# Encoder layer: where TensorE's idle warming products stand

## The chip, the cores and the metric

The kernel runs on one core of a Trainium2 chip. The metric is device time in microseconds: from one launch to its end, median over runs. One core has five engines that run their own instruction streams and wait for each other through semaphores: TensorE (PE; its weight loads are listed as PEld), VectorE (DVE), ScalarE (ACT), GpSimd (POOL) and SyncE (SP), the last of which here only issues DMAs.

## The reference

One encoder layer over a sequence of 4096 tokens of width 1024, all in float32:

```python
h = rmsnorm(x, pre_norm_g)
q, k, v, g_a, u_p, g_p = split(h @ w_in)          # 1024 -> 2304 columns
a = banded_attention(q, k, v, rel_bias, sink) * silu(g_a)   # |i-j| <= 128, 8 heads, 2 kv heads
p = multiscale_pool(u_p, pool_w, pool_scale) * silu(g_p)    # windows 2, 4, 8, 16
x = x + rmsnorm(concat(a, p) @ w_out, post_norm_g)
```

The products carry float32 as pairs of float16 (a high and a low part), three products for one: high by high, low by high, high by low.

## The kernel before, in words

The layer is worked off in two stages. The first makes the projections for the gates and the pooling channels (the columns g_p, g_a and u_p) for eight token tiles of 512 tokens and writes their results to scratch memory; it also scales and splits all weights. The second makes q, k and v, the attention and the output product. Only the very start of the first stage is touched by the change.

Every piece of work is a small function that is entered into a plan with a due time, `due(t, function, ...)`. At the end of the stage the plan is sorted by these times and each function issues its instructions in that order, so the due times alone set the order of the instructions within each engine's stream. They are not times at which anything runs: an instruction runs when it is at the head of its engine's stream and what it waits for is done.

The start, in the order of its data:

- SP loads the gain `g_pre`, four blocks of 128 tokens of x, and the weight tiles 0 and 2 (`x_load` L191, `w_load` L353).
- `gain_square` (L366) makes `gg`, the squared gain, on VectorE. `w_square_raw` (L406) squares a raw weight tile on ScalarE, and `w_norm_raw` (L415) lets TensorE sum these squares with `gg` as the stationary operand: 8 products of 128 x 128 for each of the two weight tiles. From their maximum `pair_scale` (L132 to L148) makes the power of two by which the weights are scaled.
- `row_prod` (L615) is one float32 product on TensorE for the attention's relative bias; `row_keep` (L619) copies it out of its PSUM buffer.
- `w_high` (L482, ScalarE) and `w_low` (L485, VectorE) write the two float16 parts of a scaled weight tile into `wa`.
- `x_high` (L224, ScalarE) and `x_low` (L231, VectorE) write the two parts of a normalised token block, and `x_turn` (L238) has SP issue the DMA that transposes it into `xt`.
- `mm_block(si, i)` (L926) makes the product of weight tile `si` with token block `i`: 24 products of 128 x 128 with 128 moving columns. The order is (0, 0), (0, 1), (2, 0), (2, 1), then, once token block 2 has been turned, (0, 2), (2, 2), (0, 3), and a last (2, 3). These eight blocks are the first products of the layer proper.

`warm_up` (L908) is neither input nor output of any of this. It multiplies constant ones with a part of `gg` and leaves the result in a PSUM buffer that nobody reads. It shares three PSUM buffers (the tag "wup") with the bias product and with the products of `u_prod` (L387), which come later. Its stationary operand `ones16` is set by VectorE with the kernel's first instructions (L161).

In the plan, `w_norm_raw` is due at 10.4 and 11.5, `row_prod` at 11.7, `warm_up` at 11.8 and the first `mm_block` at 16.3.

## Time and profile before

| | |
|---|---|
| median of three runs | 1167.52 us (1167.19 to 1174.55) |
| the profiled execution's own time | 1169.97 us |
| its span, first to last instruction | 1168.2 us |
| mean granted TensorE clock | 0.998 |
| busy: TensorE, VectorE, ScalarE, GpSimd | 97%, 79%, 65%, 25% |

All views below are of that one profiled execution. Times in them are microseconds from the span's start; an engine's busy time is a share of the span. A timeline row gives the start, the duration, the engine, the line of the kernel, the operation with the tile it writes and the tiles it reads, their shapes, how many instructions were merged, and in brackets the idle time ahead of it and what ended it. In a row of stretches the number behind x counts the instructions that ran in the stretch, also those cut by its edges.

### The profile page before, as it was taken

The page shows a single profiled execution, that of the slowest core. Times are in us where ns is not written, and L with a number is a line of the kernel's source. Part 1 is how long each engine was busy: PE and PEld are TensorE (multiplying, and loading weights), DVE is VectorE, ACT ScalarE, POOL GpSimd, SP SyncE. Part 2 cuts the span into 40 slices and gives each one's busy share as a digit, 9 for nine tenths or more (in the row PEclk, how much of TensorE's full clock was granted, in tenths as well). Part 3 has the DMA queues.
Part 4 walks back from the last instruction along what each step waited for, and adds up shares of the span by engine and source line. Part 5 has one row for each costly group of instructions (what it writes and reads, how often), then busy time and mean ns, then how long its engine had stood idle before and what let it go on. Part 6 is the DMA issues. An engine that isn't in the chain of part 4 may idle for free.

```text
span 1168.2 us, 30455 instructions
## 1 busy us (share of the span) xinstructions
PE 1132.3 (97%) x12528; PEld 839.2 (72%) x12528; DVE 920.6 (79%) x1890; ACT 757.4 (65%) x1696; POOL 286.5 (25%) x270
## 2 busy tenths in 40 slices
PE   6999999999999999999999999999999999999997
PEld 4548888888888888887576676667666666766643
DVE  5788787778878986957887778778778778777896
ACT  5756666666565535166687767777677777777773
POOL 1000000000000000001454444454444444544322
PEclk9999999999999999999999999999999999999999
DMA  9577898786988956999899999899789889898877
GB/s 262 151 238 271 202 262 286 270 301 214 316 248 264 251 203 174 342 285 251 204 188 203 219 221 203 181 235 209 158 224 217 183 220 210 206 210 213 176 186 217
DMA packets 312635, 265.00 MB, mean 227 GB/s; under 512 B 214528, under 2 KB 275584, under 8 KB 303792
## 3 DMA queue, kind: packets, MB, share of 16 engines
q1 hardware_dynamic: 308464, 248.38, 78.2%
q0 software_dynamic: 4032, 14.68, 7.2%
q8 instruction: 98, 1.61, 0.6%
q14 instruction: 41, 0.34, 0.1%
HBM read 132.97 MB, written 79.21 MB: 182 GB/s over the span
## 4 chain that ended last, share of the span: by engine, by line
PE 43%; DMA 4%; DVE 3%; ACT 1%; issue 1%; SPq 0%; DVEq 0%; POOLq 0%; ACTq 0%
PE ms L1963 11%; PE aq_p L1750 9%; PE m L1963 8%; PE o L1831 4%; PE s L1531 4%; PE kv L1492 3%; PE kv L1712 3%; DMA xt<-x_scr 2%; DMA pt<-pn 2%; PE z L1935 1%; DVE pn L1604 1%; DVE p_all L1549 1%; PE s L1935 0%; DVE mo L2005 0%; SPq L1613 0%
## 5 line engine op out<-in xcount | busy, mean ns | idle before, releaser
L989 PEld LDWEIGHTS <-wa 128*128 128x128 f16 x3360 | 329.5, 98 | 45.9 <-issue 7.3
L989 PE MATMUL ch<-xt,wa 128*128 128x256 f16 x1920 | 214.2, 274 | 3.7 <-ACT cbig L1001 3.7
L1560 ACT ACTIVATE p_all<-p_all,nm 128x384 f32<-128x384 f32 (+1 forms) x256 | 152.4, 596 | 41.1 <-DVE nm L1549 41.1
L1604 DVE SCALAR_TENSOR_TENSOR pn<-p_all,rd,pn 128x384 f16<-128x384 f32 (+1 forms) x256 | 144.5, 624 | 37.0 <-ACT pn L1596 36.2
L1963 PE MATMUL ms<-wo,ys 128*128 128x512 f16 x720 | 165.4, 379 | 3.0 <-DVE ys L1869 0.8
L1596 ACT ACTIVATE pn<-p_all,rd 128x384 f16<-128x384 f32 (+1 forms) x256 | 134.6, 596 | 35.7 <-DVE rd L1582 16.3
L1549 DVE CUSTOM_DVE_ANT_0 p_all<-s,ybig,nsink 128x384 f32<-128x384 f32 (+1 forms) x256 | 155.7, 664 | 1.7 <-PE s L1531 1.7
L1963 PEld LDWEIGHTS <-ys 128*128 128x128 f16 x720 | 68.8, 98 | 84.0 <-issue 2.4
L1963 PE MATMUL m<-wo,y 128*128 128x512 f16 x540 | 124.0, 379 | 0.3 <-DVE mo L2005 0.2
L989 PE MATMUL cl<-xt,wa 128*128 128x256 f16 x960 | 106.9, 273 | 2.2 <-DVE cbig L1014 1.7
L1869 POOL TENSOR_TENSOR y<-yf,y 128x512 f16<-128x512 f32 x29 | 33.6, 1159 | 272.4 <-ACT y L1865 272.4
L1750 PEld LDWEIGHTS <-raw 128*128 128x128 f16 x864 | 83.3, 98 | 17.4 <-issue 4.8
L1963 PEld LDWEIGHTS <-y 128*128 128x128 f16 x540 | 51.6, 98 | 61.4 <-issue 1.5
L210 POOL TENSOR_SCALAR ssq<-ssq 128x4 f32<-128x4 f32 (+1 forms) x11 | 5.5, 500 | 349.5 <-ACT jk L201 343.6
L302 DVE TENSOR_TENSOR xt<-ybig,xt 128x1024 f16<-128x1024 f32 x56 | 67.2, 1218 | 15.3 <-ACT xt L297 15.3
L1750 PE MATMUL aq_p<-xt,raw 128*128 128x256 f16 x672 | 78.1, 273 | 0.4 <-issue 0.4
L1831 PE MATMUL o<-pt,vv 128*64 128x256 f16 x1128 | 68.4, 274 | 1.8 <-DMA pt<-pn 1.7
L1869 POOL TENSOR_TENSOR ys<-at,ys 128x512 f16<-128x512 f32 x28 | 33.8, 1208 | 147.9 <-ACT ys L1865 124.3
L1831 PEld LDWEIGHTS <-vv 128*64 128x64 f16 x1128 | 59.2, 110 | 14.3 <-issue 14.3
L1531 PE MATMUL s<-k_all,q 64*32 64x288 f16 (+7 forms) x3432 | 63.1, 265 | 1.5 <-ACT k_all L1480 1.0
L1023 ACT ACTIVATE gp<-cbig,cg 128x256 f32<-128x256 f32 x42 | 19.0, 499 | 68.7 <-DVE cbig L1014 68.7
L2000 POOL TENSOR_TENSOR mo<-mo,ybig 128x512 f32<-128x512 f32 x39 | 51.3, 1316 | 44.4 <-ACT jkb L1989 44.2
(207 smaller groups left out, 1934.1 us busy)
## 6 DMA issues: line engine op xcount, KB each, us to landing
x_scr<-xt SPq DMA_DIRECT2D x16, 1024.0 KB, 7.5
xt<-x_scr SPq DMA_DIRECT2D x16, 1024.0 KB, 9.3
xn<-in_x SPq DMA_DIRECT2D x28, 512.0 KB, 8.0
ybig<-in_xT SPq DMA_DIRECT2D x28, 512.0 KB, 6.9
y_scr<-xt SPq DMA_DIRECT2D x14, 1024.0 KB, 7.0
xt<-y_scr SPq DMA_DIRECT2D x14, 1024.0 KB
mo<-in_x POOLq DMA_DIRECT2D x28, 512.0 KB, 7.4
out<-mo SPq DMA_DIRECT2D x28, 512.0 KB
```

Of the source, the lines that this page charges most:

```text
L302: eng.tensor_tensor(out=o[:, w, 1], in0=y_view(i), in1=o[:, w, 0], op=ALU.subtract)
L989: nc.tensor.matmul(acc[:, c], wa[:, q, wi, slot * HK + k, c * P : (c + 1) * P], x[:, xi, k, :], start=(fresh and n == 0), stop=(n > 3 * 2 ...
L1531: nc.tensor.matmul(s_bank[jj][r0 : r0 + nr, gg, c0:c1], q_t[u, half][a, qi, jj, tl + r0 : tl + r0 + nr], k_all[a, ki, kc : kc + c1 - c0], ...
L1549: nc.vector.tensor_tensor_reduce(out=p_t[b, half][:, hh, :nk], in0=s_t[b, half][jj][:, gg, :nk], in1=bias[:, h, lo : lo + nk], scale=negc[ ...
L1560: nc.scalar.activation(p[:, hh, :nk], p[:, hh, :nk], AF.Exp, bias=nm_t[b, half][:, hh : hh + 1], scale=-1.0, accum_out=den_t[b, half][:, h ...
L1596: nc.scalar.activation(prob_view(b, half)[:, 0, i], p_t[b, half][:, i, :nk], AF.Copy, scale=rd_t[b, half][:, 0, i : i + 1],)
L1604: nc.vector.scalar_tensor_tensor(out=pn4[:, 1, i], in0=p_t[b, half][:, i, :nk], scalar=rd_t[b, half][:, 0, i : i + 1], in1=pn4[:, 0, i], o ...
L1750: nc.tensor.matmul(acc[:, jj], w[:, wi, jj, k, :], x[:, xi, k, :], start=(first and n == 0), stop=(last and n > 3 * 2 * HK - 3), skip_grou ...
L1831: nc.tensor.matmul(o_ps[a, 2 * half : 2 * half + 2], v[:, vi, kt, a], pt[b, half][:, pi, g, :, i, :], start=(n == 0), stop=(n == last),)
L1869: eng.tensor_tensor(out=y[:, :, 1], in0=f(u), in1=y[:, :, 0], op=ALU.subtract)
L1963: nc.tensor.matmul(z_t[u, tag], y[:, k, yi, :], wo[o][:, wi, k, :], start=(n == 0 and acc is None), stop=(n == 3 * HK - 1), skip_group_che ...
L2000: eng.tensor_tensor(out=mo, in0=mo, in1=gpost[:, cs], op=ALU.mult)
```

## The change

Two things change in `warm_up` and its place. It had been six products that stream 512 columns of `gg`; it becomes forty products that stream the 128 columns of the ones themselves, into a buffer of 128 columns. Its due time goes from 11.8 to 0.6, which puts it at the head of TensorE's stream, ahead of the norm products and of the bias product. It no longer reads `gg`.

```diff
         def warm_up():
 
-            junk = psa.tile([P, 512], F32, name="warm", tag="wup", bufs=3)
-            for n in range(6):
-                nc.tensor.matmul(junk, ones16, gg[:, :4], start=(n == 0), stop=(n == 5))
+            junk = psa.tile([P, P], F32, name="warm", tag="wup", bufs=3)
+            for n in range(40):
+                nc.tensor.matmul(junk, ones16, ones16, start=(n == 0), stop=(n == 39))
...
         due(11.7, row_prod)
-        due(11.8, warm_up)
+        due(0.6, warm_up)
         due(21.0, row_keep)
```

## The prediction

> **What bounds the kernel now.** I read the page first: busy shares, slices, chain that ended last.

> ```profile
> PE 1132.3 (97%) x12528; PEld 839.2 (72%) x12528; DVE 920.6 (79%) x1890; ACT 757.4 (65%) x1696; POOL 286.5 (25%) x270
> ...
> PE   6999999999999999999999999999999999999997
> ...
> PE 43%; DMA 4%; DVE 3%; ACT 1%; issue 1%; SPq 0%; DVEq 0%; POOLq 0%; ACTq 0%
> ```

> TensorE is busy for 97% of the span, and the chain is mostly its matmuls. Only the first slice (29.2 us) falls to 6 tenths, and the change lies wholly in it. So the question is whether a shift there is handed on to the rest. Next I read the timeline of TensorE over the start (start, duration, engine, line, operation, idle time before it and its releaser).

> ```profile
> 10.56 1.96 PE L415 MATMUL n<-sq,gg 128*128 128x128 bf16 x16 [10.56 <-ACT sq L406]
> 12.45 1.87 PE L615 MATMUL fp<-onehot,rbias 32*8 32x512 f32 x2
> 14.25 2.74 PE L908 MATMUL warm<-gg,ones 128*128 128x512 bf16 x6
> 16.79 6.93 PE L926 MATMUL gp<-xt,wa 128*128 128x128 f16 x96
> 24.27 4.18 PE L926 MATMUL gp<-xt,wa 128*128 128x128 f16 x72 [0.55 <-DMA xt<-cbig]
> ```

> The six warming products stand directly ahead of the first 96 products, which are four blocks of 24: channel tiles 0 and 2 with the token blocks 0 and 1. Then TensorE is out of work for 0.55 us until token block 2 has been transposed. That wait at 24.27 is the **gate of the start**: whatever is gained ahead of it must be gained against a DMA that does not depend on the warming.

> The speed of TensorE has to be read from how many products begin in a stretch, because the column of the granted clock reads 1.00 from the first microsecond on, also where the spacing is double (columns: stretch, its length, busy time and matmuls of TensorE, granted clock, DMA share, GB/s).

> ```profile
> 16.79:19.73 2.94, 2.94 (x29) 1.00 1.12 249
> 19.73:23.55 3.82, 3.82 (x71) 1.00 1.28 210
> ...
> 12.90:16.31 3.41, 3.41 (x7) 1.00 1.07 228
> ...
> 231.35:234.77 3.42, 1.35 (x13) 1.00 0.92 355
> 234.77:238.18 3.41, 3.13 (x15) 0.50 1.01 284
> 238.18:241.59 3.41, 3.41 (x34) 1.00 1.07 367
> ```

> Two or three products at the left edge of a stretch began before it. So about 27.5 began in 2.94 us, 0.107 us each, and about 68.5 in 3.82 us, 0.056 us each: the rate doubles at 19.73, in the middle of the 96. The same halving is written in the clock column later: after a stretch in which TensorE was busy for 1.35 of 3.42 us the clock is 0.50 for exactly one stretch of 3.41 us, then 1.00 again. 19.73 + 63 x 3.4133 = 234.77, so both changes lie on one grid of 3.41 us; I take it that the clock is decided once per grid stretch from how busy that stretch was. It opened after 3.13 busy of 3.41 (92%). It did not open at 16.31, although TensorE counts as busy throughout 12.90 to 16.31: that stretch held two products with 32 active rows and 8 columns, and only 2.06 us (60%) of full warming products, from 14.25.

> **The change part by part.**

> *Removed: six 512-wide products ahead of the first product.* They hold TensorE from 14.25 to 16.79, 2.54 us. What is late next? The first product needs its weight and the transpose of token block 0.

> ```profile
> 13.79 1.15 ACT L482 ACTIVATE wa<-raw,sc 128x1024 f16<-128x1024 f32 x1 [0.25 <-DVE sc L148]
> ...
> 15.01 1.28 DVE L485 SCALAR_TENSOR_TENSOR wa<-raw,sc,wa 128x1024 f16<-128x1024 f32 x1
> ...
> 9.80 1.89 SPq L238 DMA_TRANSPOSE xt<-cbig  x1
> ...
> 12.96 3.59 SPq L238 DMA_TRANSPOSE xt<-cbig  x1
> ...
> 17.51 6.26 SPq L238 DMA_TRANSPOSE xt<-cbig  x2
> ```

> The high half of the weight is written at 13.79 + 1.15 = 14.94; the low half (15.01 + 1.28 = 16.29) is wanted only after 16 products. So block 0 starts at about 15.05 instead of 16.79, if its transpose has landed. And the blocks behind it? These are the transpose's issue-to-landing time (one transpose, token block 2, has it) and the DMA packets in five short stretches; a transpose moves packets under 512 bytes, the loads larger ones.

> ```profile
> DMA to landing us min/median/max: 6.7/6.7/6.7
> ...
> DMA packets 313, 0.08 MB, mean 200 GB/s; under 512 B 313, under 2 KB 313, under 8 KB 313
> ...
> DMA packets 6, 0.02 MB, mean 61 GB/s; under 512 B 0, under 2 KB 0, under 8 KB 6
> ...
> DMA packets 449, 0.11 MB, mean 287 GB/s; under 512 B 449, under 2 KB 449, under 8 KB 449
> ...
> DMA packets 14, 0.06 MB, mean 115 GB/s; under 512 B 0, under 2 KB 0, under 8 KB 14
> ...
> DMA packets 20, 0.08 MB, mean 137 GB/s; under 512 B 0, under 2 KB 0, under 8 KB 20
> ```

> In order: 13.0 to 13.4 (block 0 moving), 14.0 to 14.4 (done), 17.0 to 17.4 (block 1 moving), 18.2 to 18.7 and 18.7 to 19.3 (done). Token block 2 landed at 17.51 + 6.7 = 24.2, which is the wait seen at 24.27. Block 0 landed between 13.4 and 16.79, where its products began; by its packets at about 14.2. Block 1 landed between 17.4 and the beginning of its products: 24 x 0.107 after 16.79, 19.35. I take **18.8**, behind the end of its packets.

> So after the change block 0 runs 15.05 to 17.62 (or from 16.5, if a transpose always took 6.7 us; nothing below changes), TensorE waits about 1.2 us for block 1, and the other 72 products run from 18.8 on. That is half a microsecond earlier than in the profile (19.35), not 1.74. At full speed they would take 72 x 0.056 = 4.0 us and end at 22.8, with 1.4 us to spare before 24.27. At half speed throughout they would end at 18.8 + 72 x 0.107 = 26.5. What counts is when the clock opens.

> *Added: forty 128-wide products in the first microseconds.* Their operand is ready when DVE has set the ones.

> ```profile
> 0.86 0.17 DVE L161 MEMSET ones<- 128x128 bf16 x1
> ...
> L908 PEld LDWEIGHTS <-ones 128*128 128x128 bf16 x6 | 0.7, 136 | 2.8 <-issue 2.8
> ...
> L415 PE MATMUL n<-sq,gg 128*128 128x128 bf16 x16 | 2.0, 307 | 10.6 <-ACT sq L406 10.6
> ```

> So they begin near 1.1; at 0.107 us each they take 4.3 us and end near 5.4, at full rate sooner. TensorE has nothing else until 10.56, so they cost nothing. The ends for the unseen length: 40 x 0.056 = 2.2 us, and, were they not overlapped at all, 40 x 0.307 = 12.3 us, ending at 13.4 and holding back the norm products queued behind them (10.56) by 2.8 us; that begins to cost from 0.237 us each. The norm products, 16 of the same shape in 1.96 us with a wait inside, say 0.12 or less, so I take 0.107. No DMA and no instruction of another engine is moved; in TensorE's own order the burst passes 16 norm products and the bias product. PSUM buffers: warming and bias product swap two of three buffers; the next taker of each comes after 29 us, long after both are read. Nothing there.

> *What the burst leaves behind.* From 5.4 to 10.56 TensorE idles for 5.2 us. In the row 231.35:234.77 an idle 2.07 us inside one grid stretch closed the clock; 5.2 us put at least 2.6 idle into one stretch, so a clock opened by the burst is closed again by about 10 us wherever the grid lies.

> [...]

> *The sum.* The clock is closed when the products begin. In this profile's grid the stretches end at 19.73 and 23.14. Between 16.31 and 19.73 TensorE would work 1.31 + 0.93 = 2.24 us (66%), close to the 60% that did not open; so it opens at 23.14. By then (23.14 - 18.8)/0.107 = 40.6 of the 72 are done; 31.4 x 0.056 = 1.76 more give 24.90, against 24.27: **+0.63 us**. The grid's place at the start is free. If a stretch must be 92% busy, the opening falls between 21.9 and 25.3, and the same sum gives +0.06 to +1.7; with a full stretch up to 25.6, +1.8. The middle is about **+0.9**.

> Is it handed on? The next waits of TensorE that another engine ends last are these.

> ```profile
> 49.77 5.14 PE L939 MATMUL a<-xt,wa 128*128 128x512 f16 x23 [0.93 <-DVE wa L485]
> ...
> 55.85 0.38 PE L426 MATMUL n<-wsq,ones 128*128 128x2 f32 x2 [0.94 <-ACT wj L422]
> ```

> The first hangs on weights scaled by a norm that TensorE made at 44.08, so the delay arrives there as well; between zero and all of it passes, and I take all.

> So the profiled execution, 1169.97 us for a span of 1168.2, becomes 1170.9. It lies 2.45 above the median of the three runs, 1167.52 (1167.19 to 1174.55). On the median: **1168.4 us**, +0.08%. A measurement of this kernel can tell about 1%, 11.7 us, from no change; this is far inside.

> **The rivals.**

> *The clock opens in time: 1167.5.* If 66% of a stretch is enough, it opens at 19.73 here, and by 21.9 in any grid, the 72 products end before 24.27, and the DMA gate gives the same time as before. For: no row lies between 60% and 92%. Against: 66% is nearer to the stretch that failed. Chance 0.29.

> *The open clock outlives the gap: 1167.3.* The norm products run at 0.056, their end comes at most 0.4 us earlier, of which ACT's wait of 0.25 before 13.79 is all that the weight and the later transposes can use: -0.25. Chance 0.03.

> *The start is TensorE-bound: 1165.8.* If the wait at 24.27 came from work that follows TensorE, all 16.79 - 15.05 = 1.74 us would be won. Against: the row names the transpose, and the 6.7 us explain it. Chance 0.05.

> ```profile
> 53.86:57.28 3.42, 2.48 (x13) 1.00 1.24 19
> 57.28:60.69 3.41, 3.41 (x18) 1.00 0.37 22
> ```

> *Slower, the clock closes in the new wait: 1169.2.* If it is open by 18.8, the 72 products end at 22.8 and TensorE idles 1.4 us, 42% of a stretch. A stretch with 61% idle closed it; the stretch 53.86 to 57.28 above, with 0.94 of 3.42 us idle (27%), was followed by one at 1.00. Then the products from 24.27 run at half rate for up to 3.41 us, a loss of 1.7. It decides from an idle share of some 45%, and needs the grid to lie so. Chance 0.08.

> **How the numbers follow.** The forecast (0.0 to +1.8) has 0.50, the rivals 0.29, 0.03, 0.05 and 0.08, and 0.05 is left for what I do not see. None of the cases reaches 1%, so nearly all falls within it: 0.02 faster, 0.95 within, 0.03 slower. The range: below, the TensorE-bound start, 1165.8; above, the same cases on an execution like the profiled one, 1169.97 + 1.8 = 1171.8, and with the closing clock 1169.97 + 1.7 + 1.8 = 1173.5. Two of the four times of before (1169.97, 1174.55) lie well over the median, so I go to 1173.0.

> **What would show it.** Right: forty short products from about 1.1, ended by 5.5; a first block from about 15.05; a wait for the transpose of block 1 until 18.8; some 30 to 60 more products at 0.107 spacing, so that the 72 end later than 24.27; the wait at 24.27 gone or the block after it late by under 2 us; everything from 60 us on shifted by one constant. Wrong: a later start of the norm products than 10.56 (burst too long), a spacing of 0.056 already at 15 us (the clock stayed open), or a change that grows along the span.

## The result

| | before | changed |
|---|---|---|
| median | 1168.26 us (1166.43 to 1174.55, 14 runs) | 1171.11 us (1168.55 to 1173.94, 14 runs) |
| ratio to before | | 1.0024 (95% interval 1.0015 to 1.0033) |
| the profiled execution: time, span | 1169.97, 1168.2 us | 1170.10, 1168.3 us |

The change makes the kernel 2.8 us slower (1.75 to 3.9), a quarter of one per cent. The two profiled executions differ by 0.13 us only: that of before lies 1.7 above its median, that of the changed kernel 1.0 below. So the pair of profiles can show what happens at the start, but not the whole difference.

This is TensorE's timeline over the start of the changed kernel.

```profile
1.09 3.73 PE L908 MATMUL warm<-ones 128*128 128x128 bf16 x40 [1.09 <-DVE ones L161]
10.61 1.96 PE L415 MATMUL n<-sq,gg 128*128 128x128 bf16 x16 [5.79 <-ACT sq L406]
12.50 1.87 PE L615 MATMUL fp<-onehot,rbias 32*8 32x512 f32 x2
15.03 2.74 PE L926 MATMUL gp<-xt,wa 128*128 128x128 f16 x24 [0.67 <-ACT wa L482]
18.86 10.82 PE L926 MATMUL gp<-xt,wa 128*128 128x128 f16 x144 [1.09 <-DMA xt<-cbig]
...
57.08 0.38 PE L426 MATMUL n<-wsq,ones 128*128 128x2 f32 x2 [0.94 <-ACT wj L422]
```

The forty products run from 1.09 to 4.82, then TensorE idles for 5.79 us. Block 0 starts at 15.03 instead of 16.79, but TensorE then waits 1.09 us for the transpose of block 1. The wait for the transpose of block 2 (0.55 before) is gone: TensorE arrives there late. The norm product (L426) which had begun at 55.85 begins at 57.08, **1.23 us late**; "late" is meant here and below against the one profiled execution of before. TensorE's speed explains it (columns: stretch, length, busy time and matmuls of TensorE, granted clock, DMA share, GB/s).

```profile
0.50:3.91 3.41, 2.82 (x27) 1.00 0.51 121
3.91:7.32 3.41, 0.91 (x16) 1.00 1.01 405
...
14.15:17.56 3.41, 2.74 (x25) 0.50 0.98 259
17.56:20.98 3.42, 2.33 (x23) 0.50 1.11 259
20.98:24.39 3.41, 3.41 (x35) 0.50 1.32 171
24.39:27.80 3.41, 3.41 (x64) 1.00 1.09 294
```

Here the burst opened the clock at 3.91: ahead of it a product takes about 0.104 us (27 in 2.82 us), behind it 0.057 (16 in 0.91 us). From there on the column goes with the spacing: 0.50 where 35 products are counted in 3.41 us, 1.00 where 64 are. The stretch from 3.91 to 7.32 holds 0.91 us of work, and the clock closes at its end, more than 3 us before the norm products. It stays closed for five stretches, 7.32 to 24.39; the column reads 0.50 in all five. Without the two or three at the left edge that began before, the products take about 0.107 us each in 20.98 to 24.39 and about 0.056 in the next stretch.

The stretch from 14.15 to 17.56 is busy for 2.74 us (80%), and the clock does not open at its end. The first 0.22 us of that are the end of the bias product; this is the same stretch for the products of `mm_block` (L926) alone:

```profile
14.15:17.56 3.41, 2.53 (x24) 0.50 0.98 259
```

What becomes of the 1.23 us? First the same view for the rest of the span, before and changed:

```profile
57.28:1160.00 1102.72, 1086.30 (x12158) 1.00 0.87 227
```

```profile
57.28:1160.00 1102.72, 1086.79 (x12164) 1.00 0.86 228
```

TensorE is busy for 0.49 us more behind the start, which is little. Next, TensorE's timeline near 149 us, before and changed:

```profile
149.17 2.78 PE L989 MATMUL cl<-xt,wa 128*128 128x256 f16 x24 [1.22 <-DVE cbig L1014]
152.03 8.02 PE L989 MATMUL ch<-xt,wa 128*128 128x256 f16 x72
```

```profile
144.76 7.16 PE L989 MATMUL cl<-xt,wa 128*128 128x256 f16 x63
152.00 8.02 PE L989 MATMUL ch<-xt,wa 128*128 128x256 f16 x72
```

Up to here the changed kernel is late by the same amount: a cast of ScalarE that waits for TensorE (L297) begins at 145.15 before and at 146.38 changed. In the kernel before, TensorE then waits 1.22 us for VectorE (L1014, which runs from 148.43 there and from 148.40 in the changed kernel). The changed kernel has no wait there, and at 152 the two are level: in this pair the whole 1.23 us are taken up. Later waits move the two against each other again: at 177.53 the kernel before waits 1.03 us for ScalarE, and the changed kernel, which does not, has begun these products at 175.90, now 1.6 us early. Near 235 both wait for ScalarE and go on 0.24 us apart, before and changed:

```profile
235.05 1.22 PE L989 MATMUL ch<-xt,wa 128*128 128x256 f16 x5 [2.35 <-ACT cbig L1001]
```

```profile
234.81 1.39 PE L989 MATMUL ch<-xt,wa 128*128 128x256 f16 x11 [3.74 <-ACT cbig L1001]
```

### The profile page after: what moved, and what is told of

Read it like the earlier page. It is cut to its first block, busy times and chain, and to the rows that moved or that the text cites. A ratio compares the mean times of both kernels' runs of the same rounds, so it can differ in the third digit from the quotient of the medians.

```text
span 1168.3 us, 30522 instructions
## 1 busy us (share of the span) xinstructions
PE 1135.4 (97%) x12562; PEld 844.1 (72%) x12562; DVE 922.0 (79%) x1890; ACT 757.7 (65%) x1696; POOL 284.9 (24%) x270
## 4 chain that ended last, share of the span: by engine, by line
PE 42%; DMA 5%; DVE 3%; ACT 1%; issue 1%; SPq 1%; DVEq 0%; POOLq 0%; ACTq 0%
PE ms L1963 11%; PE aq_p L1750 8%; PE m L1963 8%; DMA xt<-x_scr 4%; PE o L1831 4%; PE s L1531 4%; PE kv L1492 3%; PE kv L1712 3%; PE z L1935 1%; DMA pt<-pn 1%; DVE pn L1604 1%; DVE p_all L1549 1%; PE s L1935 0%; SPq L1613 0%; DVE mo L2005 0%
```

## The experiments

**Theory A**: the loss is the clock that is closed when block 1 begins; the early burst has no part in it, since it is forgotten by 10 us. **Rivals**: the burst itself costs (B); the form costs, forty short instead of six wide (E); a delay at the start grows on the way (C) or is taken up (D); block 0's early start costs (F). All ratios are to runs of the kernel before that belong to the same comparison.

| run | what is different | ratio (95%) | the norm product of 55.85 begins at |
|---|---|---|---|
| changed kernel | | 1.0024 (1.0015 to 1.0033) | 57.08 |
| e1_none | no warming at all | 1.0026 (1.0013 to 1.0038) | 56.95 |
| e2_both | early burst and the six wide ones | 0.9999 (0.9989 to 1.0009) | 56.39 |
| e3_short_old | forty short ones, old place | 1.0003 (0.9990 to 1.0016) | 56.87 |
| e5_late32 | before, 32 more behind the fourth block | 1.0014 (1.0004 to 1.0025) | 56.47 |
| e5_late64 | the same, 64 | 1.0020 (1.0010 to 1.0030) | 57.64 |
| e8_late180 | the same, 180 | 1.0053 (1.0034 to 1.0072) | 64.67 |
| e6_fill_wait | changed, 12 full products in the wait for block 1 | 0.9990 (0.9975 to 1.0005) | 56.11 |
| e10_thin | changed, 12 thin products there | 1.0015 (1.0001 to 1.0030) | 58.84 |
| e7_open | TensorE filled from 1.1 us on | 1.0004 (0.9989 to 1.0019) | 58.75 |
| e9_again | changed kernel again | 1.0020 (1.0009 to 1.0031) | 56.52 |
| e9_look2, e9_look3 | changed kernel, one execution each | 1171.26, 1173.12 us | 55.90, 56.21 |

### No warming, and both

```diff
-        due(11.8, warm_up)
```

> The warming products are taken out altogether. Theory A (the clock is closed when the products begin, and the early burst has no part in it): TensorE behaves as in the changed kernel, block 0 from 15.0, a wait for block 1 until 18.9, the clock opens between 21.9 and 25.6, the second norm product after the start (57.08 in the changed kernel, 55.85 before) between 55.9 and 57.7; time as the changed kernel, about 1171, ratio to before 1.0015 to 1.0033. Rival B (the forty products, their place or their instructions cost something themselves): the time falls back to that of before, 1168.3, ratio 0.999 to 1.001.

Without any warming the ratio is that of the changed kernel, 1.0026. The medians say less: 1171.37 us of 12 runs against 1170.56 us of 35, only 0.8 us apart; the means are 2.5 us apart, since four of the 12 runs lie between 1174 and 1177. TensorE's stretches in the profile:

```profile
17.11:20.53 3.42, 2.30 (x23) 1.00 1.14 271
20.53:23.94 3.41, 3.41 (x35) 1.00 1.16 228
23.94:27.36 3.42, 3.42 (x64) 1.00 1.21 171
```

The clock opens at 23.94, as late as in the changed kernel (the column reads 1.00 ahead of it too, so the opening is read from the counts, 35 products and then 64). So the early burst is worth nothing here: without it the clock opens no later, at 23.94 against 24.39.

```diff
+        due(0.6, warm_early)      # the forty products
         due(11.8, warm_up)        # the six wide ones
```

> The forty early products are added and the six wide ones stay where they were. Theory A: as before, the first product at 16.8, the clock open between 17.7 and 21.1, the wait for the transpose at 24.27 still there, ratio 0.999 to 1.001. Rival B (the early burst itself costs): as the changed kernel, ratio 1.0015 to 1.0033.

0.9999: the burst costs nothing either, B falls. So what the changed kernel lacks is the six wide products just ahead of block 0. In this execution the transpose of block 2 came late, as its timeline shows:

```profile
24.78 4.18 PE L932 MATMUL gp<-xt,wa 128*128 128x128 f16 x72 [1.59 <-DMA xt<-cbig]
```

And the three stretches around that wait:

```profile
18.63:22.05 3.42, 3.42 (x64) 1.00 1.31 163
22.05:25.46 3.41, 1.81 (x34) 1.00 0.98 207
25.46:28.87 3.41, 3.41 (x64) 1.00 0.98 249
```

The clock opened at 18.63 and stayed open although TensorE was busy for only 1.81 of 3.41 us (53%).

### The form alone

```diff
-            for n in range(6):
-                nc.tensor.matmul(junk, ones16, gg[:, :4], ...)
+            for n in range(40):
+                nc.tensor.matmul(junk, ones16, ones16, ...)
```

> Only the form changes: the forty 128-wide products stand at the old place, behind the bias product. Theory A (what counts is whether TensorE is dense in the microseconds before the 72 products of blocks 1 and on): dense from 14.3, the burst ends between 17.9 and 18.6, the clock opens between 17.1 and 20.9, the 72 products end between 23.5 and 25.0, so 0 to +0.8 us, ratio 0.9995 to 1.001. Rival E (the form is what costs, 40 short instead of 6 wide): as the changed kernel, ratio 1.0015 to 1.0033.

1.0003: the place costs, not the form, though the interval (to 1.0016) just touches what E expects. The norm product is 1.02 us late in this profile, more than the 0 to 0.8 us that I expected.

### A delay of known size

```diff
         due(11.8, warm_up)
+        due(21.0, fill, 32)       # 64, 180: idle products behind the fourth block
```

> The kernel before with 32 idle products of 128 columns between the fourth and the fifth block: 32 x 0.056 = 1.8 us of work at 23.5, of which 0.55 to 0.7 fill the wait for the transpose; the rest, 1.1 to 1.2 us, is a delay of known size at 24.27 with the clock open. Handed on whole: ratio 1.0010, 1169.4. Rival C (a delay at the start grows on the way, since the changed kernel is 2.8 slower by the median with 1.2 in the one profile): 1170.5 or more, ratio 1.002 or more. Rival D (later waits take it up): under 0.5 us, ratio below 1.0005.

> The same with 64 idle products: 64 x 0.056 = 3.6 us, a delay of 2.9 to 3.0 us at 24.27. Handed on whole: ratio 1.0025, 1171.2. Rival C (it grows): 1173 or more, ratio 1.004 or more. Rival D (taken up later): below 1169.3, ratio below 1.001.

> The kernel before with 180 idle products of 128 columns between the fourth and the fifth block, 10.0 us of work and a delay of 9.3 to 9.5 us at 24.27 with the clock open. Handed on whole: 1.0081, +9.4 us. If later waits take up a fixed part of a delay (0 to 1.5 us): 1.0068 to 1.0081. Rival C (a delay grows on the way, by half or to the double as the median of the changed kernel suggests): 1.012 or more.

The two small ones came out at +1.6 us (0.5 to 2.9) and +2.3 us (1.2 to 3.5). Their delays were less than I had worked out, 0.62 and 1.79 us at the norm product, because TensorE was ready earlier than in the profile before: with 64, the idle products could begin at 22.48 already. With intervals this wide they part nothing but the extremes. The large one does; TensorE's timeline:

```profile
23.03 10.21 PE L908 MATMUL fill<-ones 128*128 128x128 bf16 x180
33.08 3.12 PE L932 MATMUL gp<-xt,wa 128*128 128x128 f16 x53
```

The fifth block began at 33.08 instead of 24.27, 8.8 us late with the clock open (180 idle products in 10.21 us, 0.057 each), and the time rose by 6.2 us (4.0 to 8.4). This delay did not grow, C falls. The wait near 235 does not take it up, as the same product in this run shows:

```profile
243.19 3.15 PE L995 MATMUL ch<-xt,wa 128*128 128x256 f16 x14 [3.31 <-ACT cbig L1007]
```

TensorE still waits there, and goes on at 243.19 instead of 235.05: 8.1 of the 8.8 us are left. Where the remainder goes is not shown. That some of the delay is taken up at all is likely, not certain, since the interval reaches up to 8.4 us.

### Closing the gap in front of block 1

```diff
         due(0.6, warm_up)
+        due(17.0, fill, 12)       # between mm_block(0, 0) and mm_block(0, 1)
```

> The changed kernel, and 12 idle products of 128 columns between block 0 and block 1, into the wait for the transpose (17.7 to 18.9). Block 0 still starts at 15.0. Theory A: from 15.0 on TensorE is dense, the clock opens between 17.8 and 21.2 instead of between 21.7 and 25.2, the 72 products end by 24.3, the delay at the norm product of 57 us is under 0.3 us, ratio 0.999 to 1.001. Rival F (block 0's early start or the missing wide products cost in another way): ratio 1.0015 to 1.0033 as the changed kernel.

TensorE's stretches:

```profile
15.75:19.16 3.41, 3.41 (x33) 0.50 1.28 261
19.16:22.57 3.41, 2.09 (x38) 1.00 1.03 250
```

With the twelve idle products the loss is gone, 0.9990. Block 0 still starts early (15.17), so F falls. The clock opens at 19.16, while TensorE is still waiting for block 1, which landed late in this execution (its products begin at 20.51, in the changed kernel's profile at 18.86).

The last doubt was whether the products must be full. The thin ones have 32 active rows and 8 columns, the shape of the bias product, and last about as long (1.44 us for the twelve, 1.49 for the full ones):

```diff
+                nc.tensor.matmul(junk[:8], ones16[:32, :8], ones16[:32], ...)   # 12 times
```

> As the run that filled the wait for block 1 with 12 idle products (ratio 0.999, 0.9975 to 1.0005), but with 32 active rows and 8 columns instead of 128 and 128, the shape of the bias product. TensorE is as busy by the profile, 17.7 to 19.0. Theory A (the clock opens by how dense the full products are, and the bias product's shape does not count): the clock opens as in the changed kernel, between 22.0 and 24.6, or near 18 where the grid lies so that block 0 fills a stretch to three quarters; ratio 1.001 to 1.003. Rival G (what helped was that TensorE had something to issue, not what it computed): the clock opens between 17.8 and 21.2, ratio 0.998 to 1.0005.

TensorE's stretches:

```profile
15.50:18.91 3.41, 3.41 (x34) 0.50 1.22 288
18.91:22.33 3.42, 1.68 (x17) 0.50 0.99 201
22.33:25.74 3.41, 3.41 (x34) 0.50 1.18 235
25.74:29.15 3.41, 3.41 (x64) 1.00 0.94 299
```

By the profile TensorE is busy without a break from 15.50 to 18.91, and the clock does not open at 18.91; in the run with full products a stretch just as busy opened it. Only 2.39 of the 3.41 us are products of block 0, less than the 2.53 us that did not open the changed kernel's clock either. The clock opened two stretches later, at 25.74, and 1.0015 lies on the side of the changed kernel, though its interval touches 1.0001. The two runs' intervals overlap a little; the opening is the sharper evidence. Block 1 landed late here too (21.00), which adds to the delay of 2.99 us.

### Keeping the clock open all the way

```diff
-        due(0.6, warm_up)
+        due(0.6, fill, 120)
+        due(11.8, fill, 30)
+        due(17.0, fill, 31)
```

> Idle products fill nearly all of TensorE's idle time up to block 1: 120 short ones from 1.1, 30 between the bias product and block 0, 31 between block 0 and block 1. If the clock stays open from 4 or 7 us on, the norm products take 0.056 instead of 0.107 and the weight is there 0.25 us earlier; the 72 products end at about 23 and the transpose of block 2 gates as before: 0 to -0.3 us, ratio 0.9990 to 1.0005. If the clock closes again in the norm and bias products, as the changed kernel or a little later, ratio 1.0015 or more.

TensorE's timeline, the rows of the norm products and of the first block behind the transpose of block 2:

```profile
10.51 0.61 PE L415 MATMUL n<-sq,gg 128*128 128x128 bf16 x8
...
25.54 5.81 PE L932 MATMUL gp<-xt,wa 128*128 128x128 f16 x72 [2.03 <-DMA xt<-cbig]
```

The stretches there:

```profile
19.86:23.28 3.42, 3.42 (x65) 1.00 1.26 134
23.28:26.69 3.41, 1.38 (x26) 1.00 1.15 236
26.69:30.11 3.42, 3.42 (x36) 0.50 0.95 270
```

By the grid (23.28 less five stretches) the clock opened at 6.21, and it stayed open: the 120 idle products took 9.30 us (12.8 at 0.107 each), the first eight norm products 0.61 us (before, fifteen are counted in the first 1.65). It brought nothing that can be measured, 1.0004 (0.9989 to 1.0019): TensorE got to the transpose of block 2 early and waited 2.03 us, and a stretch with 1.38 of 3.41 us of work closed the clock right behind that wait. The norm product is 2.90 us late in this execution, more than in any profile of the changed kernel, and the ratio does not show it. None of the runs beats the kernel before beyond its interval.

### The changed kernel again

> The changed kernel once more. If the loss is only the late opening of the clock at the start, as far as it is handed on, the time is 0.5 to 1.8 us over that of before, ratio 1.0004 to 1.0015, and the first comparison (1.0024) was at the edge of what it shows. If there is a second loss, the ratio is again 1.002 to 1.003. The grid of the clock lies elsewhere: it opens for the products between 21.7 and 25.2, and the norm product of 57 us comes between 55.9 and 57.7, the later the later it opens.

> The changed kernel, one look: another place of the grid. Opening between 21.7 and 25.2; the delay of the norm product of 57 us against 55.85 is 0.48 x (opening - 21.8), zero to 1.7 us, plus what the transpose of block 2 lands later.

> As the look before, a third place of the grid, by the same formula.

The loss is there a second time, 1.0020; by the expectation, that is the case of a second loss beside the late opening. In the three profiles the clock opened for the products at 22.85, 18.45 and 18.65: two of three outside the span that I had given. The stretches of the second:

```profile
15.04:18.45 3.41, 2.74 (x24) 0.50 1.22 272
18.45:21.87 3.42, 3.05 (x55) 1.00 1.05 265
21.87:25.28 3.41, 2.10 (x39) 1.00 1.22 171
```

And the stretch of the third that opened the clock:

```profile
15.24:18.65 3.41, 2.69 (x24) 0.50 1.23 278
```

The second's timeline at the transpose of block 2:

```profile
24.31 4.18 PE L926 MATMUL gp<-xt,wa 128*128 128x128 f16 x72 [1.31 <-DMA xt<-cbig]
```

In the second the grid began a stretch just as block 0 began, 2.74 of 3.41 us (80%), all of full products, were enough, and TensorE waited for the transpose as before: no delay (55.90). In the first profile of the changed kernel the same 2.74 us, 0.22 of them of the bias product, were not enough. So the delay at the start differed with the place of the grid: the four profiles opened at 24.39, 22.85, 18.45 and 18.65 and have 1.23, 0.67, 0.05 and 0.36 us.

## Why the prediction was right or wrong

- **Direction and size.** The forecast was 1168.4, +0.9 us on the median, with a range of 1165.8 to 1173.0. The result, 1171.11, is within the range, and the change is small and the way that was forecast. The size was too small: 2.8 us (1.75 to 3.9) against 0.9.
- **The removed products.** Right: block 0 at 15.03 (15.05 forecast), the wait for block 1 until 18.86 (18.8). The gain at the next gate is nothing, because the transpose of block 2 comes no earlier (24.31 and 24.63 in the two later profiles that wait for it, 24.27 before).
- **The added burst.** Right: it begins at 1.09 and ends at 4.8, costs nothing that can be measured (0.9999 with both) and leaves nothing. The clock that it opened at 3.91 was closed at 7.32.
- **When the clock opens.** The step that it opens one stretch late held in the changed kernel's profile (24.39; the delay 1.23 lies in my 0.0 to 1.8), and in the profile without warming (23.94). The bound of it was wrong: I put the limit at about 92% of a stretch, these runs put it between 74% and 79% for full products (2.53 of 3.41 us did not open in the changed kernel's first profile, 2.69 did in the third of its later ones). So the rival in which the clock opens in time is no rival of the whole but the case of some executions, two of the four profiles.
- **"Is it handed on? I take all."** The sum has two terms, the delay at the start and the share of it that is handed on, and neither explains the size. The delay was within what I gave, 1.23 us in the first profile and 0.6 in the mean of four. The share is not one number: nothing of 1.23 us in the profiled pair, about 6.2 of 8.8 us (4.0 to 8.4) with the large added delay. Even handed on whole, 0.6 to 1.2 us is not 2.8.
- **What is left open.** The four comparisons of kernels that open late in some or all executions (1.0024, 1.0020, 1.0026, 1.0015) average 1.0021, the three that can open in time (0.9999, 1.0003, 0.9990) 0.9997: 2.8 us apart. With the run that kept the clock open (1.0004) on the second side it is 2.6. So dense full products in front of the first blocks go with the lower time; how the time is lost without them is not shown. The delays at the norm product do not sort the runs: the profiles of the late ones average 1.07 us, those of the three 0.61, and with the fourth 1.18. **One to two microseconds are not located.** They are hardly a fixed cost of the burst or of the form (0.9999 and 1.0003), nor more work on TensorE behind 57 us in the profiled pair (1086.30 and 1086.79). A single profile cannot show them: the two single executions of the changed kernel differ by 1.9 us in time and by 0.3 us in that delay.
- **The rivals.** The open clock that outlives the gap: no; 0.91 us of work in the stretch closed it. The start bound by TensorE: no; its waits at 18.86, and at 24.31 in the second of the later profiles, were ended by the transposes. The clock that closes in the new wait: not in the changed kernel, whose clock stayed open after a stretch with 2.10 of 3.41 us, but it came true in the run that kept the clock open (1.38 of 3.41).
- **When the clock closes.** The reading of 231.35 to 234.77, that 2.07 us of idle time inside one stretch close the clock, held: stretches of 3.41 us with 0.91 us of work (changed kernel), 1.35 (before) and 1.38 (the run that kept the clock open) closed it, those with 1.81 (both kinds of warming) and 2.10 (the second of the later profiles) did not.

## What to carry to other kernels

In these runs warming products were worth something only where they stood directly in front of the first blocks or between them (0.9999, 1.0003 and 0.9990, against 1.0024 and, without any, 1.0026); 5.79 us of idle time behind them undid them. Whether a stretch was dense enough had to be read from the matmuls in it, with the shape of each product in view: a stretch busy for 3.41 of 3.41 us, about 1.02 of them on products of 32 rows by 8 columns, did not open the clock. Where a transfer gated the start anyway, warming was there to arrive at that gate in time, and more of it brought nothing (1.0004, with a wait of 2.03 us at the gate). And a delay that one profile shows at the start is no forecast of the time: the next wait on another engine may take it up whole, as the 1.22 us at 149 us did here.
